# Memory-attention heads of a hybrid decoder step, taken in pairs, with TensorE's and the issue queue's order written out through their two rounds

## The chip, the core and the metric

The kernel is one launch on one core of a Trainium2 chip. A core has five engines with instruction streams of their own: TensorE (PE, matrix products into PSUM), VectorE (DVE), ScalarE (ACT), GpSimd (POOL) and SyncE (SP). In this kernel SP does nothing but issue transfers (DMAs), in the order of its stream, and an engine whose next instruction waits does not go on to the one behind it. The metric is the device time of the launch in microseconds; smaller is better.

## The reference

One layer of a decoder step on a prompt of 2048 tokens and on 32 sample tokens. The normed input is projected once; the projection's columns feed a gated convolution, eight dilated-window attention heads, four memory-attention heads and a gate. The three results are joined, gated, projected by `w_out` (1024 to 1024), added to the input and normed. What the change touches is the memory attention of the prompt, four heads of 64 columns over 256 memory tokens:

```
def _mem_attn(qm, mk, mv):
    s = jnp.einsum('bthe,bmhe->bhtm', qm, mk, preferred_element_type=F32) * (HEAD_DIM ** -0.5)
    p = jax.nn.softmax(s, axis=-1)
    return jnp.einsum('bhtm,bmhe->bthe', p, mv.astype(F32))
...
    mix = mix * jax.nn.silu(z)
    return x + mix @ w_out
```

All of it is in float32. The kernel keeps that accuracy by splitting an operand into a high and a low part (`qh`, `ql`; `woh`, `wol`; `mh`, `ml`) and adding the products of the parts.

## The kernel before

The launch has three stages. First come the projections, whose results (queries `dq_hi`, `dq_lo`, keys, gate `dz`) go to DRAM. Then come the heads, one unit after the other: eight windowed heads (`Head`), then four memory heads (`MemHead`). Last comes the output stage (`Rows`): 17 blocks of tokens times `w_out`, with rows 2 to 15 at the end in one dense run of products.

A unit has two halves. `scores` multiplies its keys with all 2048 queries (on PE, `qk`, two products for each PSUM buffer, high and low part of the query), copies (memory head, ACT) or biases (windowed head, DVE) them into SBUF, and takes for every query the greatest score over each 32 keys (`Maxima.add`, on DVE). `Maxima.finish(half)` makes of that a row maximum `Rm` for 1024 queries: a reduction on DVE, a transpose on PE, a reduction on DVE, a small write to DRAM (`dmax`) and a load that spreads it over 128 partitions (`Rm`, 512 KB). `values` then subtracts `Rm` from the scores on POOL, takes the exponential on ACT, multiplies with the values on PE into `acc`, adds up the denominators on PE (`Sums`), copies `acc` to `o_sb` on ACT, and in `finish_head` divides by the denominators (ACT copy, four transposes, reciprocal on DVE, widening on ACT, eight transposes, two products on DVE) and writes `o_sb` to `dmix` in DRAM. The output stage loads it from there.

A unit uses one of two sets of buffers, by its `turn`: `keys[turn]` (`qh`, `ql`, `ks`, `kr`) and `vals[turn]` (`Rm`, `S`, `SS`, `S3`, `v1` to `v3`). A memory head uses only a part of a set. The scores of a unit run beside the values of the unit before it; this is a round. In a round `period` deals out steps: the scores in `n` equal steps, and the values and the loads at the places that they `yield` (0.25 is a quarter of the round). `acc` and `o_sb` (the tile `osb`) exist once and three PSUM buffers serve the scores (`psQ`).

Under `manual_schedule` the instructions of the engines named stay in the order in which the program writes them; elsewhere a scheduler orders each engine by priorities and times that it assumes. Before, PE and SP are under it for the rounds of heads 1 to 7 only. The rounds of the memory heads, the last two memory heads' values and the start of the output stage are ordered by the scheduler. ACT, DVE and POOL are ordered by the scheduler everywhere. `load_wo` brings `w_out` in 16 pieces of 256 KB and splits each (ACT makes `woh`, DVE or POOL `wol`).

Of the kernel before, what the change touches and what calls it, by code (L numbers as in the profile page):

```python
# [19 lines left out]
T = 2048  # L20
NS = 32
NR = T + NS
H = 8
# [251 lines left out]
def tile_step(ctx, tc, x_prompt, x_sample, mem_prompt, ck, cv, cconv, cmk, cmv, g_in, w_in, conv_w,  # L275
# [450 lines left out]
    class Maxima:  # L726


        def __init__(self, turn, Rm, n):
# [20 lines left out]
    class Sums:  # L750


        def __init__(self):
            self.ps = psP.tile([128, 4, 128], F, name="pp")
            self.first = [True] * 4

        def add(self, g, c0, n, weights, last=False):
            out = self.ps.rearrange("p a b -> p (a b)")[32 * g:32 * g + 32, c0:c0 + n]
# [5 lines left out]
    def finish_head(o_sb, sums, row, at):  # L764

        rx = wk.tile([128, 16, 64], F, name="rx", bufs=1)
# [229 lines left out]
    class MemHead:  # L996
        def __init__(self, h, turn):
            self.h, self.turn = h, turn

        def load_qk(self):  # L1000
            h = self.h
            self.q = q_load(512 + h * 64, self.turn)
            self.mk = mk = keys[self.turn].tile([128, T], R, name="ks").rearrange("p (a b) -> p a b", b=128)[:, 0:2]
# [3 lines left out]
        def load_v(self):  # L1007
            pass

        def regroup(self, d, parts):  # L1010
            pass

        def scores(self):
            vp, mk, (qh, ql) = vals[self.turn], self.mk, self.q
            Rm = vp.tile([128, T], F, name="Rm")
            mx = Maxima(self.turn, Rm, 2)
            S = {}
            for hf in range(2):
                for kb in range(2):
                    S[kb, hf] = vp.tile([128, 8, 128], F, name="S", bufs=4)  # L1020
                for q in range(2):
                    for kb in range(2):
# [7 lines left out]
            self.S, self.Rm = S, Rm.rearrange("p (r b) -> p r b", b=128)  # L1030
            for hf in range(2):
                mx.finish(hf)
                yield

        def values(self):
            h, S, Rm = self.h, self.S, self.Rm
# [258 lines left out]
```

## Time and profile before

| what | value |
|---|---|
| median of 3 runs (lowest to highest) | 1369.4 us (1365.25 to 1371.61) |
| the profiled execution's own time | 1372.67 us |
| its span, first to last instruction | 1370.6 us |
| busy in the span: PE, DVE, ACT, POOL | 91%, 47%, 32%, 33% |
| mean granted clock of PE | 0.961 of full speed |

The profiled execution takes 2.1 us more than its span, and is 3.3 us above the median. A share of busy time is a mean over stages with different limits, so it does not say what bounds a stage. The memory heads' work lies between about 1063 us (first scores) and 1185 us (last values) of the span, the output stage from 1166 us to the end.

### The profile page before, as it was taken

Reading aid. Unit: us, or ns where it says so; the run is one execution under the profiler, and the core shown is the slowest. Engines: PE = TensorE matmul, PEld = TensorE weight load, DVE = VectorE, ACT = ScalarE, POOL = GpSimd, SP = SyncE. Lnnn points to the kernel's source line nnn. Section 1 sums busy time; section 2 is a strip of 40 time slices with the busy share of each in tenths; the row PEclk is TensorE's granted clock in tenths of the full one; section 3 lists DMA queues with packets and bytes.
Section 4 is the critical chain, followed back from the end, with each engine's and each line's share of the span. In section 5 each row is a group of like instructions: output and inputs, shape, how many; then the busy total and the mean of one; then the engine's idle time right before and its main releaser. Section 6 shows DMA issues by size and latency. Waiting matters only on the chain. (4 is left out here: it accounts for less than half of the span.)

```text
span 1370.6 us, 20158 instructions
## 1 busy us (share of the span) xinstructions
PE 1241.9 (91%) x7814; PEld 1000.6 (73%) x7814; DVE 643.0 (47%) x1201; ACT 436.6 (32%) x692; POOL 458.9 (33%) x398
## 2 busy tenths in 40 slices
PE   6999999988899999999999938889889877999997
PEld 5778898977788777778887936666667442678886
DVE  4555121466556612301640437777777235554442
ACT  5433032223232010011122225556665465421111
POOL 3120010355556201101640014666666565110000
PEclk9999999999999999999999969999999989999999
DMA  6453142477887246575546357888887846876641
GB/s 230 131 154 104 41 145 87 169 260 244 268 259 253 74 96 160 158 190 176 162 151 157 86 123 169 173 183 186 185 185 164 204 112 186 240 218 202 190 155 70
DMA packets 228102, 229.56 MB, mean 167 GB/s; under 512 B 67348, under 2 KB 182280, under 8 KB 223912
## 3 DMA queue, kind: packets, MB, share of 16 engines
q1 hardware_dynamic: 216488, 207.30, 55.9%
q10 hardware_dynamic: 11520, 20.98, 4.1%
q8 instruction: 62, 1.02, 0.3%
q14 instruction: 32, 0.26, 0.1%
HBM read 171.92 MB, written 56.31 MB: 167 GB/s over the span
## 5 line engine op out<-in xcount | busy, mean ns | idle before, releaser
L359 PE MATMUL b<-hA_hi,whi 128*128 128x384 f32 (+1 forms) x576 | 191.4, 332 | 13.7 <-ACT big L607 11.4
L359 PE MATMUL b<-hA_hi,wlo 128*128 128x384 f32 (+1 forms) x576 | 189.0, 328 | 0.0
L359 PE MATMUL b<-hA_lo,whi 128*128 128x384 f32 (+1 forms) x576 | 188.6, 327 | 0.0
L351 POOL TENSOR_TENSOR wlo<-wraw,whi 128x512 fp32r<-128x512 f32 x56 | 80.9, 1461 | 295.5 <-ACT whi L350 294.8
L359 PE MATMUL b<-hB_hi,whi 128*128 128x512 f32 (+1 forms) x416 | 164.1, 394 | 9.7 <-ACT big L607 2.0
L124 POOL TENSOR_TENSOR spr<-sk,sqb 128x512 f32<-128x512 f32 (+2 forms) x110 | 121.7, 1117 | 127.1 <-DMA sqb<-dqs 43.3
L359 PE MATMUL b<-hB_lo,whi 128*128 128x512 f32 (+1 forms) x416 | 163.1, 392 | 0.0
L359 PE MATMUL b<-hB_hi,wlo 128*128 128x512 f32 (+1 forms) x416 | 162.8, 391 | 0.0
L359 PEld LDWEIGHTS b<-hA_hi,whi 128*128 128x128 f32 x576 | 110.2, 191 | 20.0 <-ACT big L607 12.3
L125 DVE TENSOR_REDUCE sc<-spr 128x8 f32<-128x512 f32 (+1 forms) x160 | 88.4, 572 | 73.7 <-POOL spr L124 73.3
L795 DVE SCALAR_TENSOR_TENSOR S<-dt,b 128x128 f32<-128x128 f32 (+2 forms) x224 | 70.1, 355 | 103.6 <-PE b L792 69.7
L359 PEld LDWEIGHTS b<-hA_hi,wlo 128*128 128x128 f32 x576 | 110.1, 191 | 4.1 <-issue 3.3
L359 PEld LDWEIGHTS b<-hA_lo,whi 128*128 128x128 f32 x576 | 110.0, 191 | 2.9 <-issue 2.9
L1198 PE MATMUL b<-woh,mh 128*128 128x512 f32 x256 | 99.9, 393 | 5.0 <-DVE xo L1228 3.3
L409 POOL TENSOR_TENSOR ss<-ss,nhalf 128x1 f32<-128x1 f32 (+1 forms) x34 | 20.8, 613 | 243.9 <-DVE ss L408 235.0
L1198 PE MATMUL b<-woh,ml 128*128 128x512 f32 x256 | 100.4, 394 | 0.2 <-DVE ml L1190 0.2
L359 PEld LDWEIGHTS b<-hB_hi,whi 128*128 128x128 f32 x416 | 79.2, 190 | 28.1 <-issue 3.2
L1198 PE MATMUL b<-wol,mh 128*128 128x512 f32 x256 | 98.7, 389 | 0.0
L928 POOL TENSOR_TENSOR S<-S,Rm 128x512 f32<-128x512 f32 x32 | 40.3, 1281 | 170.3 <-DMA Rm<-dmax 146.4
L828 ACT ACTIVATE kr<-ks 128x512 fp32r<-128x512 f32 x64 | 69.0, 1117 | 79.8 <-PE b L792 63.8
L791 PE MATMUL b<-qh,kr 128*128 128x256 f32 x256 | 75.1, 323 | 21.4 <-DMA qh<-dq_hi 20.9
L359 PEld LDWEIGHTS b<-hB_lo,whi 128*128 128x128 f32 x416 | 79.2, 190 | 19.8 <-issue 3.3
(234 smaller groups left out, 2370.1 us busy)
## 6 DMA issues: line engine op xcount, KB each, us to landing
sk<-in_cache_win_k_dram SPq DMA_DIRECT2D x72, 256.0 KB, 4.1
vq<-in_cache_win_v_dram SPq DMA_DIRECT2D x36, 512.0 KB, 4.1
wraw<-in_w_in_dram SPq DMA_DIRECT2D x48, 256.0 KB, 3.7
sqb<-dqs SPq DMA_DIRECT2D x48, 256.0 KB, 4.3
qh<-dq_hi SPq DMA_DIRECT2D x24, 512.0 KB, 10.4
ql<-dq_lo SPq DMA_DIRECT2D x24, 512.0 KB, 10.6
Rm<-dmax SPq DMA_DIRECT2D x24, 512.0 KB, 4.4
v<-out_dram SPq DMA_DIRECT2D x16, 512.0 KB, 17.8
```

What stands on the lines that cost most here:

```text
L124: E.tensor_mul(pr[:n, :width], kt, qt)
L125: nc.vector.tensor_reduce(dst, pr[:n, :width].rearrange("p (h e) -> p h e", e=64), axis=AX.X, op=OP.add)
L351: lo_eng.tensor_sub(lo[:, a:a + 4], raw, f32(hi[:, a:a + 4]))
L359: nc.tensor.matmul(ps, a(d), b(d), start=(n == 0), stop=(n == 23))
L409: nc.gpsimd.tensor_tensor(ss[:n], ss[:n], nhalf[:n], op=OP.pow)
L791: nc.tensor.matmul(out, keys, a, start=True, stop=False)
L795: nc.vector.scalar_tensor_tensor(S, dt, sl, ps, op0=OP.mult, op1=OP.add)
L828: nc.scalar.activation(self.kr[:, r4 * 512:(r4 + 1) * 512].rearrange("p (a b) -> p a b", a=d // 4), src[:, r4], AF.Copy)
L928: nc.gpsimd.tensor_sub(S3[:, r4], S3[:, r4], mr[:, r4])
L1198: nc.tensor.matmul(self.ps[k], l[:, d], r[d][:, sl], start=first and i == 0, stop=last and i == 2)
```

## The change

Four memory heads in four rounds become two pairs in two rounds. A pair uses one set of buffers: its first head those that a memory head used, its second head those that a windowed head uses besides (`ks` and `kr` for its queries, `S3` for its row maximum, `SS` for its scores). The first head's `o_sb` and widened denominators lie in `v1` and `v2`, the second's still in the shared `osb` and `rx`. The first half's row maximum is asked for while the second half's scores run, the second half's behind the next head's first scores (or, for the second head, at 0.1 of the next round). The two rounds are written under `manual_schedule`, so PE's and SP's order in them is the program's. All 16 pieces of `w_out` are asked for ahead of the last pair's values. The numbers of products, copies, subtractions and exponentials do not change.

```
--- before.py
+++ after.py
@@ -710,23 +710,26 @@
-    def q_load(row, turn):
-        qh = keys[turn].tile([128, T], R, name="qh")
-        ql = keys[turn].tile([128, T], R, name="ql")
+    def q_load(row, turn, hi="qh", lo="ql"):
+        qh = keys[turn].tile([128, T], R, name=hi)
+        ql = keys[turn].tile([128, T], R, name=lo)
...
-    dmax = [dr.tile([64, 32], F, name="dmax%d" % i) for i in range(2)]
+    dmax = [dr.tile([64, 32], F, name="dmax%d" % i) for i in range(4)]
...
-        def __init__(self, turn, Rm, n):
+        def __init__(self, turn, Rm, n, parts=None):
+            if parts is not None:
+                self.parts, self.Rm, self.n, self.d = parts, Rm, n, dmax[2 + turn]
+                return
...
-    def finish_head(o_sb, sums, row, at):
-
-        rx = wk.tile([128, 16, 64], F, name="rx", bufs=1)
+    def finish_head(o_sb, sums, row, at, rx=None):
+
+        if rx is None:
+            rx = wk.tile([128, 16, 64], F, name="rx", bufs=1)
...
     class MemHead:
-        def __init__(self, h, turn):
-            self.h, self.turn = h, turn
+
+
+        def __init__(self, h, turn, second):
+            self.h, self.turn, self.second = h, turn, second
 
         def load_qk(self):
-            h = self.h
-            self.q = q_load(512 + h * 64, self.turn)
-            self.mk = mk = keys[self.turn].tile([128, T], R, name="ks").rearrange("p (a b) -> p a b", b=128)[:, 0:2]
+            h, kp = self.h, keys[self.turn]
+            self.q = q_load(512 + h * 64, self.turn, *(("ks", "kr") if self.second else ("qh", "ql")))
+            self.mk = mk = kp.tile([128, 2, 128], R, name="mk%d" % self.second)
...
         def scores(self):
             vp, mk, (qh, ql) = vals[self.turn], self.mk, self.q
-            Rm = vp.tile([128, T], F, name="Rm")
-            mx = Maxima(self.turn, Rm, 2)
             S = {}
+            if self.second:
+                Rm = vp.tile([128, T], F, name="S3")
...
+                SS = vp.tile([128, 4, 8, 128], F, name="SS")
...
                         nc.scalar.activation(S[kb, hf][:, 4 * q:4 * q + 4], ps, AF.Copy)
+                    if hf and q == 0:
+                        mx.finish(0)
+                    if q:
+                        for kb in range(2):
+                            mx.add(mx.parts[:, 32 * hf:32 * hf + 32, kb], S[kb, hf].rearrange("p r (x c) -> p (r x) c", c=32))
                     yield
-                for kb in range(2):
-                    mx.add(mx.parts[:, 32 * hf:32 * hf + 32, kb], S[kb, hf].rearrange("p r (x c) -> p (r x) c", c=32))
...
-            for hf in range(2):
-                mx.finish(hf)
-                yield
...
             for hf in range(2):
+                if hf and self.second:
+                    yield 0.1
+                    self.mx.finish(1)
                 for kb in range(2):
                     nc.gpsimd.tensor_sub(S[kb, hf], S[kb, hf], Rm[:, 8 * hf:8 * hf + 8])
                     nc.scalar.activation(S[kb, hf], S[kb, hf], AF.Exp)
-                yield 0.25 + 0.4 * hf
+            for hf in range(2):
+                yield (0.42, 0.62, 0.84, 1.05)[2 * self.second + hf]
+                if hf == 0:
+                    sums = Sums()
+                    po = psA.tile([128, 2, 512], F, name="acc")
+                    if own:
+                        o_sb = vp.tile([128, 16, 64], F, name="v1").rearrange("p (a r) b -> p a (r b)", r=2)
+                    else:
+                        o_sb = wk.tile([128, 8, 128], F, name="osb", bufs=1)
...
-            yield from finish_head(o_sb, sums, 768 + h * 64, 1.2)
+            yield from finish_head(o_sb, sums, 768 + h * 64, 0.74 + 0.43 * self.second,
+                                   vp.tile([128, 16, 64], F, name="v2") if own else None)
+
+    class MemPair:
+        def __init__(self, h, turn):
+            self.heads = [MemHead(h + i, turn, i) for i in range(2)]
...
+        def scores(self):
+            first, second = self.heads
+            yield from first.scores()
+            for i, _ in enumerate(second.scores()):
+                if i == 0:
+                    first.mx.finish(1)
+                yield
+
+        def values(self):
+            steps = [[next(g), g] for g in [x.values() for x in self.heads]]
+            while steps:
+                x = min(steps, key=lambda y: y[0])
+                yield x[0]
+                x[0] = next(x[1], None)
+                if x[0] is None:
+                    steps.remove(x)
...
-    units = [Head(h, h % 2) for h in range(H)] + [MemHead(h, h % 2) for h in range(HM)]
+    units = [Head(h, h % 2) for h in range(H)] + [MemPair(0, 0), MemPair(2, 1)]
...
     with tc.manual_schedule(engines={mybir.EngineType.PE, mybir.EngineType.SP}):
         periods(1, H, 24)
-    periods(H, len(units) - 1, 6)
-    advance(9.0)
-    with tc.high_priority(350):
-        for _ in units[-1].scores():
-            pass
+        periods(H, H + 1, 22)
+        periods(H + 1, H + 2, 16)
+        advance(9.0)
     p2q.close()
...
     with tc.high_priority(100):
-        lw = load_wo()
-        for _ in range(8):
-            next(lw)
-    interleave(units[-2].values(), lw, 6, 16)
+        for _ in load_wo():
+            pass
     p2v.close()
```

Three places in the engines' streams show what moves. The first is SP's, in the rounds of the memory heads. `dmax` and then `Rm` (or, for a pair's second head, `S3`) is the way of one row maximum; `qh`, `ql`, `ks`, `kr` from `dq` are query loads of 512 KB; `dmix<-osb` is a head's output. Before:

```order
L748 DMA Rm_9108<-dmax1_6299 128x1024
L747 DMA dmax1_6299<-mc_9543 32x32
L717 DMA qh_9805<-dq_hi_66 64x2048
L748 DMA Rm_9108<-dmax1_6299 128x1024
L747 DMA dmax0_6298<-mc_9662 32x32
L718 DMA ql_9806<-dq_lo_67 64x2048
L717 DMA qh_9805<-dq_hi_66 64x2048
L718 DMA ql_9806<-dq_lo_67 64x2048
L1004 DMA ks_9811<-dmk_hi_70 64x256
L747 DMA dmax0_6298<-mc_9698 32x32
```

In the change, behind four row maxima (two of head 7, two of the first memory head) and the first four of the second pair's eight query loads:

```order
L717 DMA ks_9656<-dq_hi_66 64x2048
L718 DMA kr_9657<-dq_lo_67 64x2048
L717 DMA ks_9656<-dq_hi_66 64x2048
L718 DMA kr_9657<-dq_lo_67 64x2048
L1011 DMA mk1_9662<-dmk_hi_70 64x256
L1012 DMA mk1_9662<-dmk_lo_71 64x256
L750 DMA dmax2_6300<-mc_9695 32x32
L751 DMA S3_9628<-dmax2_6300 128x1024
L793 DMA dmix_73<-osb_9555 64x8x128 x2
L750 DMA dmax2_6300<-mc_9872 32x32
L751 DMA S3_9628<-dmax2_6300 128x1024
L750 DMA dmax1_6299<-mc_9904 32x32
```

Query loads stood between row maxima, four at a time; now all eight of a pair stand together, behind the row maxima that are ready early and ahead of those of the second head (`dmax2`), with head 6's output behind these.

The second place is POOL's, where head 7's subtractions (`SS`) end and the memory heads' (`S<-S,Rm`) begin. Before:

```order
L944 TENSOR_TENSOR SS_9110<-SS_9110,Rm_9108 128x12x32
L1043 TENSOR_TENSOR S_9510<-S_9510,Rm_9509 128x1024
L1043 TENSOR_TENSOR S_9511<-S_9511,Rm_9509 128x1024
L1043 TENSOR_TENSOR S_9608<-S_9608,Rm_9509 128x1024
L1043 TENSOR_TENSOR S_9609<-S_9609,Rm_9509 128x1024
L1043 TENSOR_TENSOR S_9758<-S_9758,Rm_9757 128x1024
L1043 TENSOR_TENSOR S_9759<-S_9759,Rm_9757 128x1024
```

In the change:

```order
L949 TENSOR_TENSOR SS_9111<-SS_9111,Rm_9109 128x12x32
L1052 TENSOR_TENSOR S_9558<-S_9558,Rm_9518 128x1024
L1052 TENSOR_TENSOR S_9559<-S_9559,Rm_9518 128x1024
L1052 TENSOR_TENSOR SS_9630<-SS_9630,S3_9628 128x1024 x4
L1052 TENSOR_TENSOR S_9829<-S_9829,Rm_9828 128x1024
L1052 TENSOR_TENSOR S_9830<-S_9830,Rm_9828 128x1024
L1052 TENSOR_TENSOR S_9890<-S_9890,Rm_9828 128x1024
L1052 TENSOR_TENSOR S_9891<-S_9891,Rm_9828 128x1024
L1052 TENSOR_TENSOR SS_9928<-SS_9928,S3_9926 128x1024 x2
L1202 TENSOR_TENSOR wol0_10106<-woraw_10107,woh0_10105 128x512
L1052 TENSOR_TENSOR SS_9928<-SS_9928,S3_9926 128x1024 x2
```

The first head's first two subtractions (`S_9519`, `S_9520`) have moved up into the middle of head 7's; the order of the rest and their number are as before.

The third place is ACT's, around the last two exponentials of the memory heads (`SS_9928` or `S_10060`, `S_10061`) and the first split of a joined block for the output stage (`mh`). Before, with three exponentials:

```order
L1044 ACTIVATE S_10041<-S_10041 128x1024
L1189 ACTIVATE mh_10249<-mx_10247 128x1024
L1044 ACTIVATE S_10060<-S_10060 128x1024
L1151 ACTIVATE woh2_10111<-woraw_10133 128x512
L1151 ACTIVATE woh2_10111<-woraw_10137 128x512
L1044 ACTIVATE S_10061<-S_10061 128x1024
L1189 ACTIVATE mh_10329<-mx_10327 128x896
```

In the change:

```order
L1053 ACTIVATE SS_9928<-SS_9928 128x1024
L1069 ACTIVATE osb_10027<-acc_10026 128x4x128
L1053 ACTIVATE SS_9928<-SS_9928 128x1024
L1201 ACTIVATE woh4_10097<-woraw_10139 128x512
L774 ACTIVATE rx_10061<-b0_10052 128x512
L1201 ACTIVATE woh4_10097<-woraw_10143 128x512
L1201 ACTIVATE woh5_10095<-woraw_10147 128x512
L1069 ACTIVATE v1_10319<-acc_10318 128x4x128
L783 ACTIVATE rx_10061<-rl_10068 128x1024
L1201 ACTIVATE woh5_10095<-woraw_10151 128x512
L1069 ACTIVATE v1_10319<-acc_10318 128x4x128
L1237 ACTIVATE mh_10191<-mx_10189 128x1024
```

The split `mh` of the first output block stood ahead of the last two exponentials and now stands nine instructions behind the last one, together with the copies of `acc` and of the denominators of the two heads before the last. On PE the first output products (L1198, now L1246) stood between the sums of the last head, and now stand behind the products and sums of three heads and half of the fourth's products.

## Rows read from the trace of the kernel before

**Rows 1.** The page's first part: busy us, share of span, instructions.

```profile
PE 1241.9 (91%) x7814; PEld 1000.6 (73%) x7814; DVE 643.0 (47%) x1201; ACT 436.6 (32%) x692; POOL 458.9 (33%) x398
```

**Rows 2.** Busy time by stretches, with granted clock (PEclk), DMA share and rate.

```profile
core 0: us, PE busy (x) PEld busy (x) DVE busy (x) ACT busy (x) POOL busy (x), PEclk, DMA share, GB/s
1040.00:1060.00 20.00, 18.04 (x172) 13.38 (x172) 16.27 (x31) 10.54 (x15) 17.82 (x16) 0.91 1.03 206
1060.00:1063.00 3.00, 3.00 (x49) 2.66 (x45) 2.16 (x5) 0.00 (x0) 0.00 (x0) 1.00 0.03 5
...
1075.00:1090.00 15.00, 11.12 (x74) 6.73 (x78) 3.55 (x7) 6.70 (x10) 13.57 (x12) 0.77 1.02 252
...
1105.00:1125.00 20.00, 11.48 (x81) 5.48 (x77) 4.42 (x8) 10.56 (x15) 10.32 (x5) 0.83 0.63 156
...
1200.00:1363.00 163.00, 159.69 (x697) 130.47 (x696) 73.35 (x88) 30.56 (x44) 10.27 (x15) 1.00 0.54 172
```

**Rows 3.** The chain that ended last, its end: start, length, what.

```profile
1231.37 121.11 PE b L1198 x528
1352.47 11.00 PE b L1208 x48
```

**Rows 4.** PE in order of time: start, length, what, idle before and releaser.

```profile
1107.51 1.94 PE L1048 MATMUL acc<-S,memv 128*64 128x512 f32 x8
1109.38 0.66 PE L774 MATMUL b<-ident,rx 128*128 128x128 f32 x4
...
1113.03 1.92 PE L761 MATMUL b<-S,ones 128*32 128x512 f32 x16 [0.40 <-DVE osb L785]
...
1122.69 0.79 PE L791 MATMUL b<-qh,ks 128*128 128x512 f32 x1 [6.62 <-ACT S L1026]
...
1165.82 0.73 PE L1198 MATMUL b<-woh,mh 128*128 128x512 f32 x2 [1.72 <-ACT mh L1189]
```

**Rows 5.** POOL in order of time, from head 7's first subtraction to the last.

```profile
1076.43 2.49 POOL L928 TENSOR_TENSOR S<-S,Rm 128x512 f32<-128x512 f32 x2 [18.61 <-DMA Rm<-dmax]
...
1099.66 9.38 POOL L1043 TENSOR_TENSOR S<-S,Rm 128x1024 f32<-128x1024 f32 x4
1118.73 9.30 POOL L1043 TENSOR_TENSOR S<-S,Rm 128x1024 f32<-128x1024 f32 x4 [9.68 <-DMA Rm<-dmax]
1134.70 4.67 POOL L1043 TENSOR_TENSOR S<-S,Rm 128x1024 f32<-128x1024 f32 x2 [6.68 <-DMA Rm<-dmax]
1141.34 4.72 POOL L1043 TENSOR_TENSOR S<-S,Rm 128x1024 f32<-128x1024 f32 x2 [1.96 <-DMA Rm<-dmax]
1154.76 5.18 POOL L1043 TENSOR_TENSOR S<-S,Rm 128x1024 f32<-128x1024 f32 x2 [8.71 <-DVE rl L777]
1159.90 1.72 POOL L1152 TENSOR_TENSOR wol<-woraw,woh 128x512 fp32r<-128x512 f32 x1
1161.59 5.32 POOL L1043 TENSOR_TENSOR S<-S,Rm 128x1024 f32<-128x1024 f32 x2
```

**Rows 6.** Groups by line and form, 1063 to 1200 us: POOL's and ACT's costliest.

```profile
L1043 POOL TENSOR_TENSOR S<-S,Rm 128x1024 f32<-128x1024 f32 x16 | 38.6, 2436 | 27.0 <-DMA Rm<-dmax 18.3 <-DVE rl L777 8.7
```

**Rows 7.** SP's issues in order of time: a row maximum's way, twice.

```profile
1063.54 0.53 SPq L747 DMA_DIRECT2D dmax<-mc  x1
...
1067.94 0.35 SPq L748 DMA_DIRECT2D Rm<-dmax  x1
...
1129.37 0.32 SPq L747 DMA_DIRECT2D dmax<-mc  x1
1130.75 0.33 SPq L748 DMA_DIRECT2D Rm<-dmax  x1
```

**Rows 8.** ACT in order of time, two places in the memory heads' stretch.

```profile
1121.10 1.06 ACT L1044 ACTIVATE S<-S 128x1024 f32<-128x1024 f32 x1 [5.88 <-POOL S L1043]
1122.06 0.58 ACT L1026 ACTIVATE S<-b 128x512 f32<-128x512 f32 x1
...
1151.17 0.60 ACT L1051 ACTIVATE osb<-acc 128x512 f32<-128x512 f32 x1 [2.85 <-DMA dmix<-osb]
```

More of the change, by code (lines that the diff above doesn't have):

```diff
@@ L753, in __init__ @@
         def __init__(self):
-            self.ps = psP.tile([128, 4, 128], F, name="pp")
-            self.first = [True] * 4
+            self.ps, self.first = None, [True] * 4
         def add(self, g, c0, n, weights, last=False):
+            if self.ps is None:
+                self.ps = psP.tile([128, 4, 128], F, name="pp")
             out = self.ps.rearrange("p a b -> p (a b)")[32 * g:32 * g + 32, c0:c0 + n]
@@ L1026, in scores @@
                         nc.scalar.activation(S[kb, hf][:, 4 * q:4 * q + 4], ps, AF.Copy)
+                    if hf and q == 0:
[3 more added lines that the diff above has]
+                            mx.add(mx.parts[:, 32 * hf:32 * hf + 32, kb], S[kb, hf].rearrange("p r (x c) -> p (r x) c", c=32))
                     yield
-                for kb in range(2):
-                    mx.add(mx.parts[:, 32 * hf:32 * hf + 32, kb], S[kb, hf].rearrange("p r (x c) -> p (r x) c", c=32))
+            self.mx = mx
             self.S, self.Rm = S, Rm.rearrange("p (r b) -> p r b", b=128)
+        def values(self):
+            h, S, Rm, own, vp = self.h, self.S, self.Rm, not self.second, vals[self.turn]
+            po = o_v = o_sb = sums = None
             for hf in range(2):
-                mx.finish(hf)
-                yield
-        def values(self):
-            h, S, Rm = self.h, self.S, self.Rm
-            po = psA.tile([128, 2, 512], F, name="acc")
-            sums = Sums()
-            o_sb = wk.tile([128, 8, 128], F, name="osb", bufs=1)
-            o_v = o_sb.rearrange("p (a r) (J b) -> p r a J b", r=2, b=8)
-            for hf in range(2):
+                if hf and self.second:
+                    yield 0.1
+                    self.mx.finish(1)
                 for kb in range(2):
@@ L1054, in values, with load_qk, load_v, regroup @@
                     sums.add(r4, 0, 512, S[kb, r4 // 2][:, 4 * (r4 % 2):4 * (r4 % 2) + 4].rearrange("p x y -> p (x y)"), last=kb == 1)
-            yield from finish_head(o_sb, sums, 768 + h * 64, 1.2)
+            yield from finish_head(o_sb, sums, 768 + h * 64, 0.74 + 0.43 * self.second,
[3 more added lines that the diff above has]
+            self.heads = [MemHead(h + i, turn, i) for i in range(2)]
+        def load_qk(self):
+            for x in self.heads:
+                x.load_qk()
+        def load_v(self):
+            pass
+        def regroup(self, d, parts):
+            pass
+        def scores(self):
[5 more added lines that the diff above has]
+                yield
+        def values(self):
+            steps = [[next(g), g] for g in [x.values() for x in self.heads]]
[5 more added lines that the diff above has]
+                    steps.remove(x)
     def interleave(first, second, n1, n2):
@@ L1111, in loads @@
     def loads(n):
+        if n == len(units) - 1:
+            return
         yield 0.2
@@ L1129, in tile_step @@
         periods(1, H, 24)
-    periods(H, len(units) - 1, 6)
-    advance(9.0)
-    with tc.high_priority(350):
-        for _ in units[-1].scores():
-            pass
+        periods(H, H + 1, 22)
+        periods(H + 1, H + 2, 16)
+        advance(9.0)
     p2q.close()
@@ L1154, in tile_step @@
     with tc.high_priority(100):
-        lw = load_wo()
-        for _ in range(8):
-            next(lw)
-    interleave(units[-2].values(), lw, 6, 16)
+        for _ in load_wo():
+            pass
     p2v.close()
```

11 lines of the change are left out of this document (7 added, 4 removed).

## The prediction

> **What bounds the kernel now.** The page first: PE is busy 91% of the span [rows 1], so anything that saves time must fill or shorten PE's gaps. The stretches show where they are [rows 2]: from 1200 us PE is busy 159.7 of 163, but in 1105 to 1125, where the memory heads run, 11.5 of 20. The end of the chain of waits [rows 3] is one run of output products, 528 in 121.11 us and 48 in 11.00, 0.229 each, up to 1363.5 us. All 816 of them take 187.2 us. The first stands at 1165.82 [rows 4], so from there to PE's end are 197.7 us that hardly hold a gap. The kernel therefore ends when the first output product may start, plus about 198. What is before that is a question of the memory heads.
>
> There POOL leads [rows 5]. It begins head 7's subtractions at 1076.43, works without a gap to 1099.66, and ends the last memory subtraction at 1166.91. In these 90.5 us it works 23.2 (head 7), 38.6 (16 memory subtractions, [rows 6]) and 1.7 (one piece of `wol`), together 63.5, and waits 9.7, 6.7, 2.0 and 8.7, together 27.0. Three of the waits end with a load of `Rm`; the row names DVE for the fourth, which is no operand of the subtraction, so I count it to the row maxima too. A row maximum's way is short when DMA is quiet (written 1129.37, loaded from 1130.75 to POOL's start at 1134.70: 1.4 and 3.9 us) and long when queries load (1063.54, 1067.94 and 1076.43: 4.4 and 8.5) [rows 5, 7]. ACT stands in line as well [rows 8]: an exponential that waited 5.88 for POOL had the copy of a score buffer behind it, and PE waited 6.62 for that copy [rows 4].
>
> **The change, part by part.** No product, copy or subtraction is added or left out; the edits that only rename tiles (`mk0`, `dmax2`, `o_sb` in `v1`) cost nothing, as their work is in the 63.5 and in the 198 already.
>
> *POOL's start.* In the round of head 7's scores two more query loads of each part (2.1 MB) are asked for ahead of head 7's values. DMA is full there up to 1060 and empty after (206 and 5 GB/s) [rows 2], so they lengthen that backlog by 10 us, to 1070. Head 7's first row maximum, asked for at 1063.54, then lands behind them at about 1070.5, and its load 3.9 later, at 1074.5. Before, the same load had four query loads in its way and POOL began at 1076.43. Bounds: 1068.8 with nothing in the way (1063.54, 1.4 and 3.9), 1086 if the 10 us come on top of today's start. I take 1075.0, near the way just worked out, a gain of 1.4.
>
> *POOL's waits.* From 1075.0 the work alone ends at 1138.5. The row maxima of head 7's second half and of the first memory head go down SP's stream ahead of the eight query loads (4.2 MB), one behind the other at 1.4 + 3.9 or less, so POOL finds them in time: two memory subtractions are done inside head 7's, and at 1107.6 it has four. The eight loads start at about 1084 and take 17 us at 252 GB/s [rows 2], to 1101. Behind them come the second head's row maximum (ready 1106, POOL wants it at 1107.6: no wait), head 6's output (landed 1110), and only then ACT may write the next `osb`, which is a wait of the kind of the 2.85 us in [rows 8]; the copies of the second pair's scores stand behind it on ACT, PE's score products behind these, and their maxima behind those. Adding 1.4 and 3.9 for each, I find POOL ready and the row maximum there at 1112.4 and 1114.7, at 1119.5 and 1120.8, at 1130.4 and 1131.2, and, with the last one behind two pieces of `w_out` on SP, at 1137.4 and 1140.6. The waits are 2.3, 1.3, 0.8 and 3.2, together 7.6, for 27.0 before. POOL then ends at 1075.0 + 63.5 + 7.6 = 1146.1, 20.8 earlier. Bounds for the waits: 0 and 27.0.
>
> *From the last subtraction to the first output product.* Before, this was less than nothing: the product at 1165.82, the last subtraction's end at 1166.91. In the change's order the product stands on PE behind the products and sums of three and a half heads, and ACT holds the `acc` copies and `mh` behind the last two exponentials (third place above). So these follow one another: the exponential 1.06; a split of `w_out` and the copy of denominators 0.6 each, by the 512-wide copy of [rows 8]; four transposes 0.66; widening, as wide as the exponential, 1.06; a split and a copy of `acc` 1.2; four products 1.94; eight sums 1.92 [rows 4]. That is 9.0, and 1.4 for the reciprocal and the hand-overs, an estimate: 10.4. Bounds: -1.1 as before, and 10.4 with half a clock's products and sums on top, 3.9 more. The granted clock did fall after PE's gaps (0.77 in 1075 to 1090 [rows 2]). I take 10.4, because ACT's order is fixed; the first output product starts at 1156.5.
>
> *From there to the end.* 187.2 us of products, the stalls that are there now, and the memory heads' rest, which grows by about 1.5 (the last head's four products and its first four transposes 1.94 and 0.66 less what was left over before): 197.7 + 1.5 = 199.2. `w_out`'s pieces are hidden behind the heads as long as `woh7` is there 47 products (10.8 us) after the first; if not, each late piece costs what it is late.
>
> The sum: 1156.5 + 199.2 = 1355.7 for PE's end, against 1363.5: 7.8 us less. The profiled execution took 1372.67, so it would take 1364.9; it stands 3.3 above the median, so the median goes from 1369.4 to 1361.6.
>
> **Where the trace and the skill differ.** For the eight query loads the row gives 252 GB/s, and the sum uses it. The Trainium skill, page DMA: Bandwidth & Descriptors, section Bandwidth, has 341 GB/s for a load of 1 MB, issued from GpSimd, on a core whose neighbour is idle. By that the 4.2 MB take 12.3 us (an estimate from that page), the waits of 2.3 and 1.3 go, and the median would be 1358.0; no stretch shown here reaches it, so it bears only on the first rival.
>
> **The rivals.**
> 1. *POOL runs without a wait.* Loads land 5 us earlier than I have them, or the scores get ahead. For it: all four of my waits are under 3.3 us. Against: each later one hangs on the one before. Waits 0: the first product at 1148.9, 15.4 gained, median 1354. If the ten us behind it were hidden too, 1344.
> 2. *Nothing moves.* The tail grows to what the waits gave back: 1075.0 + 63.5 + 7.6 and 18 us behind it, as when ACT's splits wait for pieces of `w_out` between the last exponential and `mh` (two of them stand there) for 3.5 each. Median 1369.
> 3. *Slower: score copies held behind exponentials.* In a pair's rounds ACT has ten exponentials standing ahead of score copies, and PE may not pass a product that lacks its buffer, because its order is written. One such hold cost PE 6.62 us [rows 4]. Two of them, which POOL's row maxima then have to wait for, cost 13.2 and leave 1375; from one and a half of them on, the kernel is slower than 0.5%. Against: POOL has four of the sixteen subtractions done before the second pair's scores begin.
>
> **How the numbers follow.** My forecast 0.5, the rivals 0.2, 0.18 and 0.12. About 0.5% (6.85 us) is what a measurement of this kernel can tell from no change. The forecast's own range is 5 us to either side (1357 to 1367), of which some 0.6 lies beyond 0.5%: faster 0.3 + 0.2 + 0.02 = 0.52; same 0.2 + 0.15 = 0.35; slower 0.13. The range goes from rival 1 with part of its tail hidden, 1347, to near rival 3, 1373.
>
> **What would show it.** POOL's waits among the memory subtractions: under 10 us in all, for 27.0. Its last one ends near 1146. The first output product stands some 10 us behind that, with ACT's last exponential, two copies of `acc` and `mh` between, and PE's end 199 us later. Query loads of a pair in one run of about 17 us from 1084 on, and a wait of ACT's `osb` copy for `dmix` near 1107. It is wrong if POOL starts head 7 after 1080, if PE waits more than 5 us for a score copy, or if the output products start less than 5 us, or more than 15, after the last subtraction.

## The result and the profile after

The changed kernel is slower: 1390.13 us median of 4 runs (1383.66 to 1395.61) against 1370.51 us median of 4 for the kernel before (1365.25 to 1375.73). The ratio on record is 1.013 with a 95% interval of 1.0104 to 1.0156 (these two medians divided give 1.0143). The profiled execution is its lowest run, 1383.66 us with a span of 1381.6.

The first part of the page of the changed kernel hardly differs from [rows 1] (PE is busy 1239.2 us, POOL 457.4), and the stretches, taken as in [rows 2], tell where the time went:

```profile
core 0: us, PE busy (x) PEld busy (x) DVE busy (x) ACT busy (x) POOL busy (x), PEclk, DMA share, GB/s
1200.00:1363.00 163.00, 152.21 (x642) 122.90 (x641) 72.97 (x89) 30.22 (x44) 7.66 (x14) 0.96 0.59 182
1201.50:1216.00 14.50, 4.81 (x13) 2.94 (x12) 7.67 (x14) 3.98 (x7) 1.09 (x2) 0.79 0.78 216
1216.00:1229.00 13.00, 11.90 (x38) 9.06 (x39) 4.93 (x5) 1.06 (x1) 0.00 (x0) 0.71 0.99 291
```

In [rows 2] PE was busy 159.69 of the 163 us from 1200 on, and its clock full; now it is 152.21, and 27.5 us of it (1201.5 to 1229) hold only 51 products, which at 0.229 each are 11.7 us of work. PE in order of time shows what it waited for there, and what stands in its stream ahead:

```profile
1163.17 0.73 PE L1246 MATMUL b<-woh,mh 128*128 128x512 f32 x2
...
1183.45 1.92 PE L765 MATMUL b<-SS,ones 128*32 128x512 f32 x16
1190.48 0.60 PE L779 MATMUL b<-ident,rx 128*128 128x128 f32 x4
1196.87 1.03 PE L789 MATMUL b<-ident,rx 128*128 128x128 f32 x8
1204.99 0.73 PE L1246 MATMUL b<-woh,mh 128*128 128x512 f32 x2 [3.42 <-ACT mh L1237]
1216.00 1.22 PE L1246 MATMUL b<-woh,mh 128*128 128x512 f32 x2 [6.22 <-ACT mh L1237]
1218.32 0.79 PE L1246 MATMUL b<-woh,ml 128*128 128x512 f32 x1 [1.09 <-DVE ml L1238]
```

The waits are 10.7 us together, for the input of the last part of row blocks 0 and 1 and for block 2. The first of these inputs is the last memory head's output; block 2's load (1205.96) stands behind it and needs a buffer that those blocks hold. SP's issues of the changed kernel show the stores of the third head (`v`) and the fourth (`osb`), and then those of the kernel before for the same two heads:

```profile
1179.71 1.51 SPq L793 DMA_DIRECT2D dmix<-v  x2
...
1199.19 1.26 SPq L793 DMA_DIRECT2D dmix<-osb  x2
1202.53 1.31 SPq L1233 DMA_DIRECT2D mx<-dmix  x2
```

```profile
1165.13 1.31 SPq L788 DMA_DIRECT2D dmix<-osb  x2
...
1184.95 1.26 SPq L788 DMA_DIRECT2D dmix<-osb  x2
```

The chain that ended last closes as in [rows 3], 10.9 us later, PE's end being 1363.41 + 11.00 = 1374.41:

```profile
1218.32 145.09 PE b L1246 x622
1363.41 11.00 PE b L1256 x48
```

POOL in order of time, to be held against [rows 5]; the first line is window head 7, and the lines with x2 are half a memory head each:

```profile
1068.32 2.50 POOL L933 TENSOR_TENSOR S<-S,Rm 128x512 f32<-128x512 f32 x2 [15.73 <-DMA Rm<-dmax]
...
1075.14 4.71 POOL L1052 TENSOR_TENSOR S<-S,Rm 128x1024 f32<-128x1024 f32 x2
...
1096.24 4.72 POOL L1052 TENSOR_TENSOR S<-S,Rm 128x1024 f32<-128x1024 f32 x2
1110.07 4.67 POOL L1052 TENSOR_TENSOR SS<-SS,S 128x1024 f32<-128x1024 f32 x2 [9.11 <-DMA S<-dmax]
1115.58 4.70 POOL L1052 TENSOR_TENSOR SS<-SS,S 128x1024 f32<-128x1024 f32 x2 [0.84 <-DMA S<-dmax]
1122.83 9.30 POOL L1052 TENSOR_TENSOR S<-S,Rm 128x1024 f32<-128x1024 f32 x4 [2.55 <-DMA Rm<-dmax]
1133.00 4.71 POOL L1052 TENSOR_TENSOR SS<-SS,S 128x1024 f32<-128x1024 f32 x2 [0.87 <-DMA S<-dmax]
...
1143.14 5.14 POOL L1052 TENSOR_TENSOR SS<-SS,S 128x1024 f32<-128x1024 f32 x2 [3.75 <-DMA S<-dmax]
```

POOL does what the change is for. It waits 17.1 us instead of 27.0 and is through at 1148.28 instead of 1166.91. The last head's output, 18.0 us behind the last subtraction before (1184.95), now comes 50.9 us behind it.

**A clock for comparisons.** Profiles of these kernels differ by some us before they come to anything that was edited. The last of the projections' high-by-high products (line 359; here called the last projection product) stands at 798.0 in the kernel before, at 794.1 in the changed one, and between 797.4 and 806.3 in the experiments. So times are counted from it below. This view lists a line's matmuls with their first and last start (here of the kernel before):

```profile
L359 PE MATMUL b<-hA_hi,whi x576: 288/336/689, 146.7 to 798.0; 128*128 128x384 f32 x144, 128*128 128x288 f32 x48
```

and of the changed one:

```profile
L359 PE MATMUL b<-hA_hi,whi x576: 288/336/690, 145.1 to 794.1; 128*128 128x384 f32 x144, 128*128 128x288 f32 x48
```

| kernel | ratio to before (95%) | store, window head 7 | store, first memory head | last subtraction | first output product | store, last memory head | product to span's end | span's end |
|---|---|---|---|---|---|---|---|---|
| before | 1 | 317.2 | 333.7 | 368.9 | 367.8 | 387.0 | 204.8 | 572.6 |
| changed | 1.013 (1.0104 to 1.0156) | 335.3 | 349.2 | 354.2 | 369.1 | 405.1 | 218.4 | 587.5 |
| 1 early finishing | 1.0049 (1.0024 to 1.0075) | 337.4 | 350.9 | 357.0 | 374.5 | 396.5 | 207.6 | 582.1 |
| 2 before, late | 1.0213 (1.0173 to 1.0253) | 314.1 | 330.5 | 367.0 | 365.9 | 414.7 | 231.5 | 597.4 |
| 3 w_out split | 1.0116 (1.0088 to 1.0144) | 335.9 | 349.9 | 354.9 | 369.7 | 405.7 | 218.4 | 588.1 |
| 4 pairs, unwritten | 1.0138 (1.0106 to 1.0171) | 334.6 | 352.2 | 360.7 | 371.3 | 406.7 | 217.7 | 589.0 |
| 5 single, written | 1.0078 (1.0051 to 1.0104) | 305.7 | 333.8 | 376.9 | 380.0 | 397.3 | 204.8 | 584.8 |
| 6 queries later | 1.0132 (1.0111 to 1.0153) | 337.8 | 352.5 | 356.6 | 372.1 | 410.8 | 220.2 | 592.3 |
| 7 queries split | 1.0103 (1.0081 to 1.0126) | 337.5 | 351.4 | 356.0 | 370.4 | 406.4 | 218.9 | 589.3 |
| 8 = 1 and 6 | 1.005 (1.0031 to 1.0068) | 337.2 | 351.8 | 356.4 | 374.3 | 396.3 | 203.5 | 577.8 |
| 9 round of 8 | 1.0133 (1.0107 to 1.0158) | 330.2 | 351.9 | 371.9 | 370.8 | 402.1 | 215.9 | 586.7 |
| 10 = 1, 7 and 9 | 1.0086 (1.0055 to 1.0118) | 321.9 | 343.3 | 364.2 | 363.1 | 396.0 | 216.0 | 579.1 |
| 11 both rounds | 1.0013 (0.9988 to 1.0039) | 322.3 | 338.5 | 365.2 | 360.9 | 389.7 | 212.2 | 573.1 |
| 12 buffers | 1.0004 (0.998 to 1.0028) | 320.5 | 337.6 | 363.7 | 361.3 | 384.5 | 208.9 | 570.2 |

The first two lines of the table hold the whole case. Counted this way the changed kernel ends 14.9 us later: 1.3 up to the first output product, although the last subtraction is 14.7 earlier, and 13.6 behind it. Every memory head's store is 15.5 to 18.5 later.

### The profile page after: what moved, and what is told of

It reads as the page before. It is cut to its first block, busy times and chain, and to the rows that moved or that the text cites. A ratio compares the mean times of both kernels' runs of the same rounds, so it can differ in the third digit from the quotient of the medians.

```text
span 1381.6 us, 20147 instructions
## 1 busy us (share of the span) xinstructions
PE 1239.2 (90%) x7814; PEld 1002.9 (73%) x7814; DVE 642.8 (47%) x1201; ACT 436.4 (32%) x692; POOL 457.4 (33%) x398
## 5 line engine op out<-in xcount | busy, mean ns | idle before, releaser
L359 PEld LDWEIGHTS b<-hA_hi,whi 128*128 128x128 f32 x576 | 110.4, 192 | 18.7 <-ACT big L607 11.0
L1246 PE MATMUL b<-woh,mh 128*128 128x512 f32 x256 | 101.1, 398 | 9.6 <-ACT mh L1237 9.6
L1246 PE MATMUL b<-woh,ml 128*128 128x512 f32 x256 | 102.3, 400 | 1.1 <-DVE ml L1238 1.1
L1246 PE MATMUL b<-wol,mh 128*128 128x512 f32 x256 | 102.5, 400 | 0.0
L359 PEld LDWEIGHTS b<-hB_hi,whi 128*128 128x128 f32 x416 | 78.7, 189 | 28.5 <-issue 3.5
## 6 DMA issues: line engine op xcount, KB each, us to landing
v<-out_dram SPq DMA_DIRECT2D x16, 512.0 KB, 17.7
```

What stands on the lines that cost most here:

```text
L359: nc.tensor.matmul(ps, a(d), b(d), start=(n == 0), stop=(n == 23))
L1246: nc.tensor.matmul(self.ps[k], l[:, d], r[d][:, sl], start=first and i == 0, stop=last and i == 2)
```

## The experiments

**1 and 2: is the late last output the loss?** The theory: the loss is made behind the first output product, because the last head's finishing steps (row sums, two sets of transposes) stand behind 68, 90 and 116 output products on PE, and only 132 products can run without that head. The rival: it is made in the memory rounds. In the first run the steps are written out early:

```
-    interleave(units[-1].values(), first_rows(), 6, 80)
+    last = units[-1].values()
+    with tc.manual_schedule(engines={mybir.EngineType.PE}):
+        for _ in range(5):
+            next(last)
+        interleave(last, first_rows(), 24, 80)
```

> The changed kernel, with the products of the first output rows and the last pair's finishing steps written out on TensorE: the last head's row sums stand behind 42 output products instead of 68, its last transposes behind 72 instead of 116. Theory 1 (the loss is made behind the first output product: the last head's output leaves at 1199 us, the 132 products that can run without it are through at 1201, and TensorE then waits 10.7 us and runs at half clock until 1229): the last store of the head leaves near 1180 to 1185, the waits of 3.4, 6.2 and 1.1 us go, the clock stays at 1.00, and the time falls by 10 to 14 us, to a ratio of 0.999 to 1.005 with the kernel before. Theory 2 (the loss is made in the memory heads' rounds, ahead of the first product): the waits behind it move or shrink but the time stays within 4 us of the changed kernel's, a ratio of 1.010 to 1.015.

The second puts the lateness into the kernel before:

```
-    interleave(units[-1].values(), first_rows(), 6, 80)
+    last, rows = units[-1].values(), first_rows()
+    with tc.manual_schedule(engines={mybir.EngineType.PE}):
+        for g, n in ((last, 2), (rows, 22), (last, 1), (rows, 7), (last, 1), (rows, 9), (last, 3), (rows, 50)):
+            for _ in range(n):
+                next(g, None)
```

> The kernel before, with the last head's finishing written late on TensorE: its row sums behind 66 output products and its last transposes behind 114, as in the changed kernel (68 and 116). Nothing else of the change is in it. Theory 1 (a late last output is enough to lose the time): the store leaves about 7 to 8 us behind the 114th product, near 1200, TensorE waits for the first rows' last part and for the rows after them and falls to half clock, and the time grows by 7 to 13 us, a ratio of 1.005 to 1.010. Theory 2 (the loss is of the rounds ahead): within 3 us of the kernel before, a ratio of 0.998 to 1.002.

Run 1 measured 1.0049, at the upper edge of the theory's range. PE's waits from 1160 us on, by what ended them (us in total, times, longest), now show one behind the first product, the second of the two longest, and 1205 to 1220 is full at full clock:

```profile
PE acc L1066 <- ACT v L1069: 3.9, 1, 3.9
PE b L1246 <- DVE ml L1238: 2.6, 1, 2.6
```

```profile
1205.00:1220.00 15.00, 15.00 (x66) 11.91 (x64) 3.71 (x7) 1.57 (x3) 0.00 (x0) 1.00 0.80 211
```

The output stage falls from 218.4 to 207.6. Half of the gain is given back: the third head's finishing now stands ahead of the first product, which is 5.4 us later. The last store moved by 8.6, less than the 14 to 19 expected.

Run 2 lost more than expected, 1.0213. The same view of it:

```profile
PE b L1198 <- ACT mh L1189: 11.0, 3, 6.6
PE b L1198 <- ACT woh L1151: 6.5, 3, 4.1
PE b L1198 <- DVE ml L1190: 2.8, 2, 1.7
```

Of the 11.0 and 2.8 us, 1.72 and 1.71 stand at the first two products. The rest, 2.75, 6.56 and 1.10, are the theory's waits: 10.4 us behind 132 products, for the 10.7 of the changed kernel. The 28.5 us around them (1217.5 to 1246) hold 57 products, so 15.4 us are lost there. The 6.5 for pieces of `w_out` are not the theory's: ScalarE's splits come no later than in the kernel before, counted from the last projection product, but PE, its products now in a written order, waited for them, which it does nowhere in the output stage of the kernel before. So the ratio of run 2 does not price the lateness; those 15.4 us do. Run 2 shows that a late last output alone stops the output stage; run 1 shows what moving it forward gains in the changed kernel, 0.8% of the 1.3% (1.013 less 1.0049, each with some 0.26 to either side).

**3: do the sixteen w_out pieces hold the finishing?** Eight were to go back behind the last values (the second eight calls of `load_wo` behind `units[-1].values()`). The edit does not do that: the call only makes the generator, and its first step runs in `interleave`. So the eight pieces are still written ahead of the last values, and only their raised priority is gone.

> The changed kernel, with eight w_out pieces ahead of the last heads' values, as before, and the other eight behind them at ordinary priority. Theory 3 (all sixteen pieces at high priority hold ScalarE, VectorE and the issue queue, and so the heads' finishing: ScalarE waits 0.98, 1.38, 1.94 and 2.55 us for them): the first output product 3 to 5 us earlier relative to the last subtraction, and the ratio 1.005 to 1.010. Theory 1: the finishing stands behind the same counts of products, so the time stays, 1.011 to 1.015.

The scheduler gave ScalarE the splits at the same places as without the edit, and PE the same counts of products between the steps. So the run says nothing on this theory. It serves as a repeat of the changed kernel, 1.0116 against 1.013. The theory stays untested.

**4 and 5: the pairs or the written order?** Run 4 takes the two memory rounds out of the written order, run 5 writes the order out for single heads.

```
     with tc.manual_schedule(engines={mybir.EngineType.PE, mybir.EngineType.SP}):
         periods(1, H, 24)
-        periods(H, H + 1, 22)
-        periods(H + 1, H + 2, 16)
-        advance(9.0)
+    periods(H, H + 1, 22)
+    periods(H + 1, H + 2, 16)
+    advance(9.0)
```

> The changed kernel with its two memory rounds out of the written order: pairs as they are, TensorE's and the issue queue's order left to the scheduler. Theory 4 (the written order of the rounds holds TensorE and ScalarE: 11.2 us of ScalarE behind a store, 8.6 us of TensorE at the maxima's transposes): last subtraction and first output product 4 to 8 us earlier and a ratio of 1.000 to 1.006. Theory 1: the last pair's finishing is still behind some 80 to 120 output products, so the waits in the output stage stay and the ratio is 1.008 to 1.015.

```
     with tc.manual_schedule(engines={mybir.EngineType.PE, mybir.EngineType.SP}):
         periods(1, H, 24)
-    periods(H, len(units) - 1, 6)
-    advance(9.0)
-    with tc.high_priority(350):
-        for _ in units[-1].scores():
-            pass
+        periods(H, len(units) - 1, 6)
+        advance(9.0)
+        with tc.high_priority(350):
+            for _ in units[-1].scores():
+                pass
```

> The kernel before, heads one by one in their own buffers, with only the written order of TensorE and the issue queue carried on through the memory rounds. Theory 1 (the pairs delay the finishing, by one burst of loads and by four chains behind the subtractions): 0.995 to 1.004. Rival (an order written out by hand is what holds these rounds, since TensorE then waits at the maxima's transposes and scores): 1.006 to 1.015.

Run 4 gives 1.0138: pairs lose as much without the written order, and in the same stage (217.7). Run 5 gives 1.0078, and that loss lies elsewhere: its output stage is as long as before (204.8), but the first product comes 12.2 us later, because POOL waits in the middle of the heads, 17.94 us behind its first four memory subtractions and then:

```profile
1151.22 9.38 POOL L1043 TENSOR_TENSOR S<-S,Rm 128x1024 f32<-128x1024 f32 x4 [20.05 <-DMA Rm<-dmax]
```

That is its rival's range. So either half of the change loses time by itself, and the two losses do not add. The table also tells them apart at the first memory head's store: it is 18.5 us late with pairs alone, 0.1 with the written order alone.

**6, 7 and 8: the query loads.** In the changed kernel window head 6's output is stored at 1106.31, behind the second pair's queries, and ScalarE may not write the next output before that. SP's issues and ScalarE's line:

```profile
1094.57 0.44 SPq L1012 DMA_DIRECT2D mk<-dmk_lo  x1
1095.11 0.53 SPq L750 DMA_DIRECT2D dmax<-mc  x1
1105.88 0.33 SPq L751 DMA_DIRECT2D S<-dmax  x1
1106.31 1.31 SPq L793 DMA_DIRECT2D dmix<-osb  x2
```

```profile
1111.76 1.08 ACT L993 ACTIVATE osb<-acc 128x512 f32<-128x512 f32 x2 [11.23 <-DMA dmix<-osb]
```

Run 6 asks for the second pair's queries later (`yield 0.2` becomes `yield 0.2 if n < H else 0.5`), run 7 for those of its second head only, run 8 is 1 and 6 together.

> The changed kernel, with the query loads of the second pair (eight of 512 KB, four small ones) moved in the issue queue's order behind the store of window head 6 and the second memory head's first maxima; TensorE's order stays. Theory 1 (the finishing of the heads is set back there: the output of window head 6 is ready at 1088.7 us and its store leaves at 1106.3, so ScalarE stands 11.2 us at the copy for window head 7 and all four memory heads come late): the store leaves within 3 us of being ready, ScalarE's wait shrinks under 3 us, the memory heads' stores and the first output product come 7 to 11 us earlier counted from the last projection product (369 us in the changed kernel), and the ratio falls from 1.013 to 1.004 to 1.009. Rival (the 4.2 MB and not their place hold the maxima and the scores, or the finishing chain of 17 to 19 us a head sets the end alone): under 4 us, ratio 1.010 to 1.014.

> As the run before, but only the loads of the second head of the second pair move behind the store; those of its first head stay where the change put them, so the burst ahead of the store is 2.1 MB as in the kernel before. Theory 1: about half of the hold is left (store 4 to 8 us behind its being ready), ratio 1.005 to 1.010. If the first scores of the second pair wait for late queries in the run before, this one is the faster of the two by 2 to 5 us.

> The changed kernel with both edits: the second pair's query loads behind the store, and the last pair's finishing written early among the first output products. If both delays are causes and add up (8 us and 11 us of the 18): the last head's store about 30 us behind the last subtraction instead of 51, no wait of TensorE in the output stage, ratio 0.996 to 1.002. If the two are one and the same delay: no better than the better of the two alone, 1.004 to 1.006.

ScalarE's wait went as expected in run 6 (11.23 to 0.26), and nothing came of it (1.0132), since PE's scores now waited for the late queries and POOL for the maxima behind them:

```profile
1120.80 1.09 ACT L993 ACTIVATE osb<-acc 128x512 f32<-128x512 f32 x2 [0.26 <-PE acc L922]
```

```profile
1132.03 4.65 POOL L1052 TENSOR_TENSOR SS<-SS,S 128x1024 f32<-128x1024 f32 x2 [13.81 <-DMA S<-dmax]
```

Run 7's 1.0103 missed its range (1.005 to 1.010) and cannot be told from the changed kernel, nor run 8's 1.005 from run 1. The theory that this hold alone sets the heads back has fallen; the rival, that the 4.2 MB collide with something wherever they are put, has its wait in the row above.

**9 to 12: the places of the finishing steps, and all together.** In the written order window head 7's last transposes stand behind twelve of the second head's sixteen score products. Run 9 changes `periods(H + 1, H + 2, 16)` to 8, run 10 adds edits 1 and 7, run 11 changes `periods(H, H + 1, 22)` to 10 as well, run 12 adds to that a third buffer for `mx` and `zg` and writes the finishing six products apart (ratio 40 in place of 24).

> The changed kernel, with one number changed: the second pair's score steps are spread over 8 places of their period instead of 16, so that the finishing of window head 7 and of the first pair's heads is written ahead of more of the second pair's score products. In the order, the last transposes of window head 7 then stand ahead of the second head's score products instead of behind twelve of the sixteen and two maxima. Theory (the written places hold the finishing of window head 7 and all behind it; its store is at 335 us after the last projection product against 317 in the kernel before): its store 8 to 14 us earlier, the four memory heads' 6 to 14 us earlier, the waits of TensorE in the output stage 10.7 us to under 6, ratio 1.002 to 1.008. Rival (the finishing of the four heads is a chain that starts when the pair's exponentials are through, whatever the place): stores move by less than 4 us, ratio 1.010 to 1.014.

> Three edits at once on the changed kernel: the second pair's scores over 8 places, the query loads of its second head behind the store of window head 6, and the last pair's finishing written early among the first output products. If the three delays are separate and add: first output product 6 to 10 us earlier than with the early finishing alone (374 us after the last projection product), no wait in the output stage, ratio 0.994 to 0.999, faster than the kernel before. If the finishing chain is the limit: 1.002 to 1.006.

> As the run before, with the first pair's scores over 10 places instead of 22 as well, which writes the finishing of window head 6 ahead of more of the first pair's scores. If window head 6 is held by its place too, its store (312 us after the last projection product in the changed kernel, 286 in the kernel before) comes near 290 and the time falls by another 2 to 5 us, ratio 0.992 to 0.998; if not, as the run before.

> The run before (places of both rounds, split query loads, early finishing) with a third buffer for the rows' inputs of the output stage, so that the third block of rows can be loaded as soon as the last head is stored, and with the finishing steps written six products apart instead of nine or twelve. If what is left in the output stage there (waits of 3.3 us for pieces of w_out and 2.7 us for the third block's input, and the low clock behind them; 212 us of output stage against 204 to 205 in the kernel before) hangs on the late inputs: output stage 205 to 208 us, ratio 0.995 to 0.999. If it hangs on w_out, whose pieces land as before: 1.000 to 1.003.

Run 9 moved window head 7's store by 5.1 us, less than the 8 to 14 expected, and the last head's by 3.0; the ratio stayed, 1.0133. POOL, whose maxima now stand behind more finishing, ended 17.7 us later. With edits 1 and 7 beside it (run 10) it is 1.0086, no better than edit 1 alone. Only the first round's places make the difference (run 11): 1.0013, the stores in the table within 5.1 us of the kernel before. All that the change had lost is back, and nothing beyond it (0.992 to 0.998 was expected), although the first output product is 6.9 us earlier than before: the output stage is 212.2. Run 12's is 208.9; PE's longest waits in it from the first product on:

```profile
PE b L1251 <- ACT woh L1206: 3.2, 1, 3.2
PE b L1251 <- DVE ml L1243: 0.7, 1, 0.7
```

Block 2's late input was 2.7 us of run 11 and is gone, the wait for `w_out` is not; the ratio, 1.0004 (0.998 to 1.0028), is no change. No version beat the kernel before.

## Why the prediction was wrong, step by step

The sum was made to PE's end, 1355.7; measured 1374.41, 18.7 more. Counted from the last projection product it is 22.6, since this profile stands 3.9 us early there. Its steps:

| step | forecast | measured | added |
|---|---|---|---|
| last subtraction ends | 1146.1 | 1148.28 | 2.2 |
| from there to the first output product | 10.4 | 14.9 | 4.5 |
| from there to PE's end | 199.2 | 211.2 | 12.0 |

The medians are further apart (28.5) by 6.5 that the profiled execution lies under its median and 3.3 that I had taken off for the one before.

*POOL's start and waits.* The mechanism held: two memory subtractions inside head 7's, four done when POOL first waits, and the waits fell. That the step is only 2.2 off is luck, two errors of opposite sign. POOL began at 1068.32 and not at 1075.0, just below my lower bound of 1068.8 (3.9 of the 6.7 are the profile as a whole), and its waits were mis-sized, 17.1 for 7.6. The first was 9.11 where I had none: I had POOL ready for the second head's row maximum at 1107.6 and that there at 1106, but POOL was ready at 1100.96 and could start at 1110.07. The query loads moved at 210 GB/s (1083 to 1100) and not at 252, and the row maximum, which went to SP at 1095.11, took 10.7 us for its 4 KB to land behind what was left of their 4.2 MB. The Trainium skill, page DMA: Bandwidth & Descriptors, section Queues, rings and completion order, says that SP owns one ring on each of the 16 DMA engines and that each engine takes descriptors in ring order. The row agrees with that: the same 4 KB at 1127.52, with nothing ahead, was there when its load went out at 1128.94. Counted from the last projection product POOL gained 14.7 us, not 18.6.

*The tail.* 14.9 is 0.1 under the bound at which I had called the step wrong. Splits did wait for pieces of `w_out` between the last exponential and `mh` (0.98, 1.38 and 1.94 us), which was rival 2's mechanism, and PE waited for the copy of `acc` (`v`) behind one of them; ScalarE's row, and PE's up to the first output product:

```profile
1153.38 0.63 ACT L1201 ACTIVATE woh<-woraw 128x512 fp32r<-128x512 f32 x1 [1.38 <-DMA woraw<-in_w_out_dram]
```

```profile
1154.55 3.68 PE L1066 MATMUL acc<-S,memv 128*64 128x512 f32 x8 [3.45 <-ACT v L1069]
1158.16 1.36 PE L789 MATMUL b<-ident,rx 128*128 128x128 f32 x8
1159.45 1.94 PE L1066 MATMUL acc<-SS,memv 128*64 128x512 f32 x8
1161.31 1.92 PE L765 MATMUL b<-S,ones 128*32 128x512 f32 x16
```

But 1154.55 is 6.3 us behind the last subtraction, and the terms ahead of PE's products were 6.5 together, so these waits did not lengthen the step. PE's own part did: 8.6 us where the sum had 3.9. It ran the third head's products at half clock (3.68 for 1.94, granted 0.50 in 1154.5 to 1158), and eight transposes (1.36) and half of the last head's products (1.94) stand there that I had left out.

*From there to the end* is the step that failed. I wrote "the stalls that are there now, and the memory heads' rest, which grows by about 1.5", and so let the end hang on the first output product alone. Beyond the 187.2 of products that left 12.0 us; it measured 24.0, of which the heads' rest took 8.2 (38.4 less 30.2, below) and the stretch from 1201.5 to 1229 lost 15.8. Another chain ends there: the last head's store, its load as `mx`, and the first product with it, 1199.19 to 1204.99, 5.8 us. The 132 products that can do without it (48 of the sample rows and 42 of each of two row blocks) take 30.2 us at 0.229, and with the finishing steps between them lasted from 1163.17 to 1201.57. In the kernel before the store stood 19.1 us behind the first product, so by the same 5.8 it was back at 24.9, inside the 30.2. In the changed one it stands 36.0 behind and is back at 41.8, 3.4 after those 38.4, and that is PE's first wait. I had counted what is left of the last head as four products and four transposes, but the finishing of two heads was left, one behind the other, and each step of theirs stands behind another 22 to 26 products on PE.

*What I called the leader was not one.* "There POOL leads" was read from its waits [rows 5]. The memory heads' stores follow each other by 14.0, 17.5, 18.9 and 19.5 us in the changed kernel (the first from window head 7's) and by 16.5, 14.5, 18.9 and 19.8 in the kernel before, although POOL's waits fell by 9.9 us. So the finishing of a head (accumulator, sums, copies, transposes, store) keeps that pace here, and starts 15.5 us later. That this comes of the pairs and not of the written order, runs 4 and 5 show; pairs with other places for the steps (run 11) win 10.7 of it back. What sets the pace is open. The one accumulator and the two banks that all heads take in turn do not set it for the last two: run 1 has the same ones, and there these two stores follow by 14.6 and 12.1 us, once the steps stand behind fewer output products.

*The rivals.* Rival 1 is out, by 17.1 us of waits. Rival 2 has its mechanism, in part. Rival 3 had the right sign, and its two holds came: PE waited 5.06 and 5.75 us (at 1113.39) for score copies, each over the 5 that I had named as a sign of being wrong. The first copy stood behind window head 7's exponentials, which waited for POOL, the second behind the copy to `osb`:

```profile
1070.86 1.06 ACT L934 ACTIVATE S<-S 128x1024 f32<-128x1024 f32 x1 [4.35 <-POOL S L933]
...
1074.42 0.79 PE L796 MATMUL b<-ks,mk 128*128 128x512 f32 x1 [5.06 <-ACT S L1033]
```

By the way that rival 3 names, POOL's row maxima, they cost nothing at the end: the last subtraction came early all the same. Nor did the price fit the verdict: two holds of 6.62 leave 1375, 0.4% above 1369.4, and 0.5% takes 2.2 of them, not one and a half. No rival held the late last output. The hidden `w_out` was right for the changed kernel: from the first product on no product waits for it.

What is shown: the late last output stops the output stage, in the changed kernel and put alone into the kernel before, and writing it earlier gives back about 0.8% of the 1.3%. That edit and three others together (run 11) take away all of it. How the rest divides among the three is not settled, since 6, 7 and 9 did nothing clear of noise alone, and the first round's places were tried only on top of the others.

## What to carry to other kernels

A stage that begins with work for which the inputs are there has two starts: when its first product may run, and when its cover for the late inputs ends; a prediction has to price both, and the second is the last producer's store plus its way back against the products that can do without it. An engine that waits is the leader only if its waits set the pace of what is stored: look at the spacing of the stores before giving its waits a price. When a written order's units are doubled, the steps between which they are dealt out (6 to 80, 22, 16) have to be dealt out anew.

## What the runs showed of the hardware

A store of 4 KB issued behind eight loads of 512 KB in the same queue, 6.2 us after the last of them, took 10.7 us until the load that waits for it could go out (1095.11 to 1105.88); with nothing ahead it was 1.4 (1127.52 to 1128.94 in the same trace). After PE's gap of 3.42 us the granted clock was still 0.91 in 1204.9 to 1206.9 and then half, 0.50 in 1206.9 to 1209.8. After the second gap, of 6.22 us, it stayed at half for some 8 us, in which 16 products ran, and was full from 1224 on:

```profile
1216.00:1224.00 8.00, 6.91 (x16) 4.98 (x17) 3.49 (x3) 1.06 (x1) 0.00 (x0) 0.52 1.06 316
1224.00:1228.00 4.00, 4.00 (x20) 3.25 (x19) 1.23 (x1) 0.00 (x0) 0.00 (x0) 1.00 0.93 283
```

So 27.5 us that should have held 120 products lost 15.8 us: 10.7 to the waits, and the rest, 5.1, I put to the clock. And a profile drifts as a whole: kernels in which no edit touches what runs up to the last projection product had it up to 12.2 us apart, while the change moved PE's end by 10.9.
